# Low parts of the down weights by an adding DMA in a two-layer encoder on one core

## The chip, the core and the metric

The kernel runs on one core of a Trainium2 chip. The core has five engines that work side by side: TensorE (PE, matrix products), VectorE (DVE), ScalarE (ACT), GpSimd (POOL) and SyncE (SP), which here issues all DMAs; sixteen DMA engines move the bytes. The metric is device time in microseconds (us) of one execution; lower is better.

## The reference, cut to what matters

Two layers, each an FFN, a token-mixing sub-layer and a second FFN, on 256 tokens of width 1024, all in float32. The FFN:

```python
def swiglu(h, w_up, w_down):
    a, b = jnp.split(h @ w_up, 2, axis=-1)
    return (jax.nn.silu(a) * b) @ w_down          # w_up 1024 x 5632, w_down 2816 x 1024

for l in range(DEPTH):                            # DEPTH = 2
    h = rms_norm(x, ffn1_pre_g[l])
    x = x + 0.5 * rms_norm(swiglu(h, ffn1_w_up[l], ffn1_w_down[l]), ffn1_post_g[l])
    ...                                           # pooling, differential and memory attention, gates
    h = rms_norm(x, ffn2_pre_g[l])
    x = x + 0.5 * rms_norm(swiglu(h, ffn2_w_up[l], ffn2_w_down[l]), ffn2_post_g[l])
```

## The kernel before, in words

**Products in two parts.** PE multiplies in the type float32r, which keeps fewer bits of a number than float32. To lose little, every operand is split into a high part (the number rounded to float32r) and a low part (what the rounding left), and a product is the sum of high x high, high x low and low x high. So each weight has to become two tiles, `wh` and `wl`.

**Weights come in units.** All weights are packed on the host into 192 units of 128 x 2048 float32 (1 MB). `load_unit` (L99) issues a unit's DMA from SP into a tile `raw`, of which there are three buffers. `next_unit` (L103 and on) takes the oldest raw tile and makes the two parts, in two halves of 1024 columns each (four of 512 for the first five units of a stage): ACT writes the high part by a copy into float32r (L114), and DVE subtracts it from the raw weights to give the low part (L115). `wh` and `wl` have five buffers each. A raw buffer is free for the next load when both its readers are through; a weight buffer when PE has used the unit.

**The six stages.** FFN, mix, FFN for each layer. An FFN has 11 pairs of hidden columns (p = 0 to 10). For p from 2 on, the units of a pair's up weights come first (two units: `up2` at L241 for three of the stages; in the first stage `up`, L222), and then, for p = 2 to 9, the unit of the down weights of pair p - 2: `down(p - 2)`, whose products (L264, 24 of them in `rows_chunk`) are added up in four PSUM banks `acc`. So in the middle of a stage units come as up, up, down. The down units of the last three pairs come in the stage's `tail`, which ends in the norm and the residual.

**Beside the weights**, the hidden values go through ACT and DVE: `up2` copies a PSUM bank (L354), adds (L355), applies the gate function (L356), multiplies (L357) and splits the result into `hid` (L154, L155); the first stage does so by L330 and L331, PE transposes (L339), and L154, L155. In the first stage `ahead()` also prepares tables and the memory tokens (L410 to L513). POOL computes the power in the norms (L138).

**Order.** The program is written for a framework that sets semaphores by itself and plans the order of each engine's queue when the kernel is built; a few places are ordered by hand. Each engine works its queue in order: an instruction that waits holds up what stands behind it.

Of the kernel before, what the change touches and what calls it, by code (L numbers as in the profile page):

```python
# [9 lines left out]
F32 = mybir.dt.float32  # L10
F32R = mybir.dt.float32r
BF16 = mybir.dt.bfloat16
I32 = mybir.dt.int32
AF = mybir.ActivationFunctionType
ALU = mybir.AluOpType
# [30 lines left out]
def encoder_kernel(ctx, tc, x_d, xt_d, mem_d, memt_d, pos_d, w_d, gains_d, cols_d, lamv_d, poolw_d, cst_d, out_d):  # L46
    nc = tc.nc
# [15 lines left out]
    def acc_bank():  # L63
        return accp.tile([P, 512], F32, name="acc")
# [30 lines left out]
    def load_unit(parts=1):  # L95
        raw = rawp.tile([P, 2048], F32, name="raw")
        n = 2048 // parts
        for i in range(parts):
            nc.sync.dma_start(out=raw[:, i * n:(i + 1) * n], in_=w_d[nxt[0]][:, i * n:(i + 1) * n])  # L99
        nxt[0] += 1  # L100
        raws.append(raw)

    def next_unit():  # L103
        parts = 4 if fine[0] > 0 else 2
        fine[0] -= 1
        if not raws:
            load_unit()
        raw = raws.pop(0)
        h = wts.tile([P, 2048], F32R, name="wh")
        l = wts.tile([P, 2048], F32R, name="wl")  # L110
        n = 2048 // parts
        for s in range(parts):
            cs = slice(s * n, (s + 1) * n)
            high = nc.scalar.copy(out=h[:, cs], in_=raw[:, cs])  # L114
            low = nc.vector.tensor_tensor(out=l[:, cs], in0=raw[:, cs], in1=h.bitcast(F32)[:, cs], op=ALU.subtract)  # L115
            if nxt[1] < 2:
                first_low.append(low)
                first_high.append(high)
        nxt[1] += 1
        return h, l  # L120
# [133 lines left out]
    def rows_chunk(c, banks, todo, lhs_of, first, last):  # L254
        done = []
        for b in range(2):
            fs = slice(b * 512, (b + 1) * 512)
            for (w, kk) in todo:
                wh = w[0].rearrange("p (k m) -> p k m", k=2)
                wl = w[1].rearrange("p (k m) -> p k m", k=2)  # L260
                for k in range(2):
                    ah, al = lhs_of(c, kk, k)
                    for i, (a, ww) in enumerate(((ah, wh), (ah, wl), (al, wh))):
                        done.append(nc.tensor.matmul(  # L264
                            out=banks[b], lhsT=a, rhs=ww[:, k, fs],
                            start=(kk == first and k == 0 and i == 0),
                            stop=(kk == last and k == 1 and i == 2),
                        ))
        return done
# [14 lines left out]
    def ffn(i, xx, late, g_post, finish, ahead, raw_rstd=None):  # L284
# [9 lines left out]
            return hid[kk][0][:, c, k, :], hid[kk][1][:, c, k, :]  # L294

        def down(p):
            w = next_unit()
            if p == 0:
                for c in range(2):
                    acc[c] = [acc_bank(), acc_bank()]  # L300
            for c in range(2):
                rows_chunk(c, acc[c], [(w, p)], lhs_of, 0, NPR - 1)
# [42 lines left out]
        def up2(p, u):  # L345
            w = next_unit()
            banks = [ma_bank(), mb_bank()]
            for i in range(2):
                form_a2(banks[i], w, slice(i * P, (i + 1) * P), xx)
            flush()  # L350
            t = t2()
            for i in range(2):
                half = t[:, i * S:(i + 1) * S]
                nc.scalar.copy(out=half, in_=banks[i][:, S:2 * S])  # L354
                nc.vector.tensor_tensor(out=half, in0=banks[i][:, 0:S], in1=half, op=ALU.add)  # L355
            nc.scalar.activation(out=t[:, 0:S], in_=t[:, 0:S], func=AF.Silu)  # L356
            nc.vector.tensor_tensor(out=t[:, 0:S], in0=t[:, 0:S], in1=t[:, S:2 * S], op=ALU.mult)  # L357
            split(t[:, 0:S].rearrange("p (c t) -> p c t", c=2), hid[p][0][:, :, u, :], hid[p][1][:, :, u, :])

        ws = [(next_unit(), next_unit()) for _ in range(1 if raw_rstd else 2)]  # L360
        if raw_rstd:
            hs, ls = first_high, first_low
# [18 lines left out]
        for p in range(2, NPR):  # L381
            hid_pair(p)
            if raw_rstd:
                w2 = (next_unit(), next_unit())
                for c in range(2):
                    up(p, c, w2)
            else:
                for u in range(2):
                    up2(p, u)
            if p - 2 <= NPR - 4:  # L390
                down(p - 2)
            if p == 4:
                ahead()
# [529 lines left out]
```

## Time and profile before

| what | value |
|---|---|
| median of 3 runs | 1143.73 us (1143.53 to 1143.85) |
| the profiled execution | 1144.51 us, span in the trace 1142.5 us |
| granted TensorE clock, mean | 0.998 |
| PE busy | 1133.2 us, 99% of the span |
| DVE busy | 752.0 us, 66% |
| ACT busy | 626.8 us, 55% |
| POOL busy | 25.4 us, 2%, 37 instructions |
| DMA engines | 218.32 MB, mean 191 GB/s, busy 52.8% with the queue that SP feeds |

How to read it: the span is the time from the first to the last instruction in the trace; the execution's own time is about 2 us more. Busy time is what an engine spends in instructions, whether or not anyone waits for them. In the groups of the profile a row gives line, engine, operation, tiles and shapes, then the count, the busy time in us, the mean of one in ns, and the idle time of the engine just before them with what ended it. A "wait" names who waited for whom. DVE waits for the high part before 78 of its 444 subtractions, and SP's loads wait mostly for DVE, whose subtraction is the last reader of a raw buffer.

### The profile page before, as it was taken

The numbers are of one execution on the slowest core, as the hardware profiler recorded it, in microseconds if no ns is written. First come the engines' busy times: TensorE is split into PE (matmuls) and PEld (weight loads), VectorE is DVE, ScalarE is ACT, GpSimd is POOL, SyncE is SP. The second block draws the span as 40 slices with busy tenths as digits, with TensorE's granted clock in tenths as the row PEclk, the third lists the DMA queues.
The fourth block names the chain that finished last, engine by engine and source line by source line (L and its number), as shares of the span: only waits on it lengthen the run. The fifth ranks groups of instructions, "written<-read, shape, count | busy, mean of one in ns | idle before, by whom it ended". The sixth has DMA issues, their size and how long they took to land.

```text
span 1142.5 us, 14737 instructions
## 1 busy us (share of the span) xinstructions
PE 1133.2 (99%) x5679; PEld 947.5 (83%) x5679; DVE 752.0 (66%) x1164; ACT 626.8 (55%) x1121; POOL 25.4 (2%) x37
## 2 busy tenths in 40 slices
PE   8999999999999999999999999999999999999997
PEld 6888888887888888888888888888878888888886
DVE  6767456576768866566586756575677688666553
ACT  7666445545664555555565655555555646555551
POOL 0000000000000100000000000010000001000000
PEclk9999999999999999999999999999999999999999
DMA  8975553553454565555465655545545534655530
GB/s 314 341 245 223 192 188 139 211 189 120 170 205 161 212 249 195 196 184 185 148 234 208 221 188 186 185 163 202 183 147 188 199 149 171 253 184 184 185 111 37
DMA packets 35493, 218.32 MB, mean 191 GB/s; under 512 B 4192, under 2 KB 4448, under 8 KB 11232
## 3 DMA queue, kind: packets, MB, share of 16 engines
q1 hardware_dynamic: 35424, 217.40, 52.8%
q8 instruction: 44, 0.72, 0.2%
q14 instruction: 25, 0.20, 0.1%
HBM read 216.33 MB, written 1.05 MB: 190 GB/s over the span
## 4 chain that ended last, share of the span: by engine, by line
PE 98%; DVE 0%; DMA 0%; ACT 0%; issue 0%; SPq 0%; DVEq 0%; POOLq 0%; ACTq 0%
PE ma L222 37%; PE acc L264 25%; PE mb L241 13%; PE ma L241 13%; PE acc L222 2%; PE mb L222 2%; PE mb L197 1%; PE acc L617 1%; PE mb L339 1%; PE mb L495 1%; PE acc L634 1%; PE acc L675 1%; PE acc L660 1%; DMA raw<-in_w 0%; PE mb L748 0%; PE mb L560 0%
## 5 line engine op out<-in xcount | busy, mean ns | idle before, releaser
L115 DVE TENSOR_TENSOR wl<-raw,wh 128x1024 fp32r<-128x1024 f32 (+1 forms) x444 | 459.3, 1077 | 159.8 <-ACT wh L114 145.9
L114 ACT CAST wh<-raw 128x1024 fp32r<-128x1024 f32 (+1 forms) x444 | 391.5, 935 | 176.9 <-issue 102.0
L222 PE MATMUL ma<-wh,xhl 128*128 128x512 f32 x1184 | 379.6, 395 | 1.6 <-ACT wh L114 1.6
L222 PEld LDWEIGHTS ma<-wh,xhl 128*128 128x128 f32 x1184 | 221.9, 189 | 49.0 <-ACT wh L114 2.1
L222 PE MATMUL ma<-wl,xhl 128*128 128x512 f32 x592 | 233.1, 394 | 0.2 <-DVE wl L115 0.2
L264 PE MATMUL acc<-wh,hid 128*128 128x512 f32 x704 | 224.7, 391 | 0.0
L241 PE MATMUL ma<-xhl,wh 128*128 128x512 f32 x432 | 157.4, 398 | 0.0
L241 PE MATMUL mb<-xhl,wh 128*128 128x512 f32 x432 | 157.0, 397 | 0.0
L264 PEld LDWEIGHTS acc<-wh,hid 128*128 128x128 f32 x704 | 132.2, 188 | 26.2
L264 PE MATMUL acc<-wl,hid 128*128 128x512 f32 x352 | 137.1, 389 | 0.0
L222 PEld LDWEIGHTS ma<-wl,xhl 128*128 128x128 f32 x592 | 111.7, 189 | 23.8 <-issue 1.3
L241 PE MATMUL mb<-xhl,wl 128*128 128x256 f32 x432 | 112.5, 281 | 0.0
L241 PE MATMUL ma<-xhl,wl 128*128 128x256 f32 x432 | 112.4, 281 | 0.0
L241 PEld LDWEIGHTS ma<-xhl,wh 128*128 128x128 f32 x432 | 81.2, 188 | 15.8
L241 PEld LDWEIGHTS mb<-xhl,wh 128*128 128x128 f32 x432 | 81.5, 189 | 14.5
L355 DVE TENSOR_TENSOR s<-mb,s 128x256 f32<-128x256 f32 x54 | 22.9, 425 | 103.4 <-ACT s L354 103.4
L241 PEld LDWEIGHTS mb<-xhl,wl 128*128 128x128 f32 x432 | 81.6, 189 | 5.0
L241 PEld LDWEIGHTS ma<-xhl,wl 128*128 128x128 f32 x432 | 81.5, 189 | 4.6
L264 PEld LDWEIGHTS acc<-wl,hid 128*128 128x128 f32 x352 | 66.2, 188 | 13.7
L354 ACT COPY s<-mb 128x256 f32<-128x256 f32 x54 | 20.2, 373 | 58.4 <-PE mb L241 58.4
L356 ACT ACTIVATE s<-s 128x256 f32<-128x256 f32 x54 | 22.6, 418 | 50.9 <-DVE s L355 50.9
L138 POOL TENSOR_TENSOR sm<-sm,mhalf 128x1 f32<-128x1 f32 (+1 forms) x26 | 22.5, 865 | 1029.7 <-DVE sm L147 836.9
(162 smaller groups left out, 973.4 us busy)
## 6 DMA issues: line engine op xcount, KB each, us to landing
raw<-in_w SPq DMA_DIRECT2D x189, 1024.0 KB, 4.8
gain<-in_gains SPq DMA_DIRECT2D x17, 512.0 KB, 5.2
raw<-in_w SPq DMA_DIRECT2D x8, 256.0 KB, 5.5
hid<-in_memt SPq DMA_DIRECT2D x8, 256.0 KB, 5.7
hid<-in_xt SPq DMA_DIRECT2D x4, 256.0 KB, 5.3
raw<-in_w SPq DMA_DIRECT2D x2, 512.0 KB, 6.8
x<-in_x SPq DMA_DIRECT2D x4, 256.0 KB, 6.6
hid<-in_mem SPq DMA_DIRECT2D x4, 256.0 KB, 5.7
```

The source lines that it names most:

```text
L114: high = nc.scalar.copy(out=h[:, cs], in_=raw[:, cs])
L115: low = nc.vector.tensor_tensor(out=l[:, cs], in0=raw[:, cs], in1=h.bitcast(F32)[:, cs], op=ALU.subtract)
L138: nc.gpsimd.tensor_tensor(out=r, in0=v, in1=mhalf[:, :n], op=ALU.pow)
L197: tps.append(nc.tensor.transpose(out=ps[:, k * P:(k + 1) * P], in_=xn[:, i * P:(i + 1) * P], identity=ident))
L222: done.append(nc.tensor.matmul(out=out, lhsT=lhsT, rhs=rhs, start=(first and i == 0), stop=(last and i == n - 1)))
L241: nc.tensor.matmul(out=o, lhsT=ww[:, k, ms], rhs=rhs, start=(k == 0 and o is full), stop=(k == KT - 1 and o is full))
L264: done.append(nc.tensor.matmul(out=banks[b], lhsT=a, rhs=ww[:, k, fs], start=(kk == first and k == 0 and i == 0), stop=(kk == last and k = ...
L339: nc.tensor.transpose(out=tp[:, u * P:(u + 1) * P], in_=hn[:, u, :], identity=ident)
L354: nc.scalar.copy(out=half, in_=banks[i][:, S:2 * S])
L355: nc.vector.tensor_tensor(out=half, in0=banks[i][:, 0:S], in1=half, op=ALU.add)
L356: nc.scalar.activation(out=t[:, 0:S], in_=t[:, 0:S], func=AF.Silu)
L495: ins.append(nc.tensor.transpose(out=tp[:, i * P:(i + 1) * P], in_=a[:, hh, kt * P:(kt + 1) * P], identity=ident))
```

## The change

For the units that `down` fetches, 32 of the 192 (8 in each of the four FFN stages), the low part is made in another way. ACT writes the high part as before. Then ACT writes the negated high part into `wl` (a copy with scale -1), and POOL issues a DMA from `raw` to `wl`, SBUF to SBUF, that adds what it moves to what stands there. Each unit has two such halves of 128 x 1024 (512 KB). The down units of the tails, and all other units, keep the subtraction.

```diff
-    def next_unit():
+    def next_unit(added=False):
...
             high = nc.scalar.copy(out=h[:, cs], in_=raw[:, cs])
+            if added:
+                nc.scalar.activation(out=l[:, cs], in_=h.bitcast(F32)[:, cs], func=AF.Copy, scale=-1.0)
+                nc.gpsimd.dma_start(out=l[:, cs], in_=raw.bitcast(F32R)[:, cs], accum_op=ALU.add)
+                continue
             low = nc.vector.tensor_tensor(out=l[:, cs], in0=raw[:, cs], in1=h.bitcast(F32)[:, cs], op=ALU.subtract)
...
         def down(p):
-            w = next_unit()
+            w = next_unit(True)
```

## The prediction

> **What bounds the kernel now.** I read the page's busy times first, then its chain that ended last, then the longest pieces of that chain in order of time.
>
> ```profile
> span 1142.5 us, 14737 instructions
> PE 1133.2 (99%) x5679; PEld 947.5 (83%) x5679; DVE 752.0 (66%) x1164; ACT 626.8 (55%) x1121; POOL 25.4 (2%) x37
> PE 98%; DVE 0%; DMA 0%; ACT 0%; issue 0%; SPq 0%; DVEq 0%; POOLq 0%; ACTq 0%
> 0.00:7.40 7.40, 4.38 (x12) 1.52 (x12) 2.29 (x9) 4.00 (x8) 0.73 (x7) 1.00 0.65 197
> 1131.00:1142.50 11.50, 5.30 (x24) 4.05 (x22) 3.11 (x6) 1.38 (x4) 0.55 (x1) 0.92 0.24 91
> ```
>
> PE is idle for 1142.5 - 1133.2 = 9.3 us in all. The two windows (columns: length, then PE, PEld, DVE, ACT, POOL busy, clock, DMA share, GB/s) hold 3.0 us of it at the start and 6.2 us at the end, and neither stretch has a down unit that the change touches. Between them nearly nothing is left to win: a DVE that is 66% busy and behind no wait of PE can be relieved without shortening anything. So the question is only whether the longer way to a low part makes PE wait.
>
> **What the change takes away and adds.** `down` runs for p = 0 to 7 in each of four FFN stages: 32 units, two halves each, 64 halves. (The three down units of each tail call `next_unit()` without the flag.)
>
> ```profile
> L115 DVE TENSOR_TENSOR wl<-raw,wh 128x1024 fp32r<-128x1024 f32 x324 | 383.2, 1222 | 149.1 <-ACT wh L114 135.4 <-PE ma L222 8.9 <-issue 0.8
> L114 ACT CAST wh<-raw 128x1024 fp32r<-128x1024 f32 x324 | 325.2, 1052 | 171.3 <-issue 102.0 <-PE ma L222 45.6 <-PE acc L264 12.2
> q1 hardware_dynamic: 35424, 217.40, 52.8%
> raw<-in_w SPq DMA_DIRECT2D x189, 1024.0 KB, 4.8
> raw<-in_w SPq DMA_DIRECT2D x2, 512.0 KB, 6.8
> L138 POOL TENSOR_TENSOR sm<-sm,mhalf 128x1 f32<-128x1 f32 (+1 forms) x26 | 22.5, 865 | 1029.7 <-DVE sm L147 836.9 <-DVE sm L641 192.8
> L138 POOL TENSOR_TENSOR rmem<-sm,mhalf 128x1 f32<-128x1 f32 x2 | 1.1, 548 | 62.8 <-DVE sm L147 62.8
> ```
>
> DVE loses 64 x 1.22 = 78 us and ends near 674. ACT gains 64 sign flips; the nearest row is its cast of the same shape, 1.05 us, so 67 us, to 694. POOL gains 64 DMA issues. The DMA engines get 64 x 0.5 MB to write, and since an addition reads its target too, 1 MB to read for each half. None of these four sums is on PE's chain; what counts is the time from one unit's raw weights to its low part.
>
> Before, the second half of a unit is ready 3.44 us after its cast starts (below: 483.67 to 484.75 + 2.36). After, a unit takes four ACT passes of 1.05 us, 4.2 us, and then D: from the end of the last flip until the second addition has landed. No row shows D, so I bound it. The loads move 217.40 MB in 52.8% of 1142.5 us, so 1 MB (1.05 million bytes) costs all engines 2.9 us, and 4.8 - 2.9 = 1.9 us of a load is fixed. Lower end: an addition as cheap as a copy of half the bytes, 1.9 + 1.45, and 0.5 us of POOL time from its shortest row: D = 3.9 us. Upper end: the slowest landing of 512 KB in the page, 6.8 us, twice for the two reads, and the POOL row: D = 14.2 us. I take the bytes at face value: two reads of 512 KB go through the engines as 1 MB does, 4.8 us; POOL 0.9 us, its commonest row; and 0.8 us because the first half was issued only 2.1 us earlier and occupies the engines for 2.9. D = 6.5 us. This is nearest to the row of the 1 MB load, which runs 189 times, while the 6.8 row stands for two loads at the crowded start.
>
> A page weighs the same step: the Trainium skill, "Collectives: The Full Stack", section "The bandwidth ceiling: the fold count and why AG ≠ RS ≠ AR", says that the add in the DMA path costs no cycles of its own and that the second read halves the rate. By that rule D would stay at my 6.5 us; no run here shows it yet.
>
> **Where the unit stands in the steady stretch.** Units come as up, up, down; three raw buffers and five weight buffers. So a down unit always takes its raw buffer over from the down unit before it.
>
> ```profile
> 483.67 2.00 ACT L114 CAST wh<-raw 128x1024 fp32r<-128x1024 f32 x2
> 484.75 2.36 DVE L115 TENSOR_TENSOR wl<-raw,wh 128x1024 fp32r<-128x1024 f32 x2
> 487.14 0.33 SPq L99 DMA_DIRECT2D raw<-in_w  x1
> 500.38 2.00 ACT L114 CAST wh<-raw 128x1024 fp32r<-128x1024 f32 x2
> 489.00 5.45 PE acc L264 x24
> 505.72 5.45 PE acc L264 x24
> 480.00:520.00 40.00, 40.00 (x215) 34.35 (x214) 24.49 (x35) 21.17 (x35) 0.00 (x0) 1.00 0.52 186
> ```
>
> The cast at 483.67 starts when PE has left a unit and a weight buffer is free; its unit is used at 505.72 (the fifth unit on), and the second half's low part first by the fifth of its 24 matmuls, 4 x 5.45 / 24 = 0.9 us later. That is 23.0 us after the cast. The new way needs 4.2 + 6.5 = 10.7. Cover: 12.3 us, first test passed.
>
> Second test, the raw buffer. At 487.14 SP reloads it, right after the subtraction; the next cast from it is at 500.38, one period of 16.72 us after the last. After the change the round is 4.2 (ACT) + D + 4.8 (load) = 15.5 us at D = 6.5, inside 16.72; it breaks at D = 7.7. What is queued behind the new waits: on SP the load of the next unit, due a third of a period later at 487.14 + 5.6 = 492.7 and now held until 483.67 + 10.7 = 494.4, 1.7 us of the 500.38 - 487.14 - 4.8 = 8.4 that a load has to spare; on ACT the copies of PE's banks at L354, 2.1 us later, where a bank is written again only two units on, over 11 us; on POOL the norms' powers, not due before the tail. DMA share in this window is 0.52; two additions of 2.9 us per 16.72 add 0.35, to 0.87, still under 1.
>
> **Where it is tight: the first FFN stage**, where the buffers have just been filled.
>
> ```profile
> 34.54 0.33 SPq L99 DMA_DIRECT2D raw<-in_w  x1
> 33.14 2.01 ACT L114 CAST wh<-raw 128x1024 fp32r<-128x1024 f32 x2
> 36.81 0.33 SPq L99 DMA_DIRECT2D raw<-in_w  x1
> 42.91 5.47 PE acc L264 x24
> 59.74 5.47 PE acc L264 x24
> 34.00:40.00 6.00, 6.00 (x29) 4.95 (x28) 4.84 (x7) 4.11 (x7) 0.00 (x0) 1.00 0.96 373
> 90.97 0.47 ACT L330 ACTIVATE s<-ma,rst 128x256 f32<-128x256 f32 x1
> 91.48 0.48 DVE L331 SCALAR_TENSOR_TENSOR s<-ma,rst,s 128x256 f32<-128x256 f32 x1 [1.22 <-ACT s L330]
> 93.01 0.27 PE L339 MATMUL mb<-ident,s 128*128 128x128 f32 x1
> ```
>
> The first down unit is cast at 33.14, flipped by 37.3, and its second half is wanted at 42.91 + 0.9 = 43.8: D may be 6.5 at most, exactly what I estimate, while the engines are 0.96 busy with the load issued at 34.54. Sharing with that load costs up to half of one half's 2.9 us; I take 1.0 us of PE wait. The raw buffer, reloaded at 36.81 before, is now free at 44.8; the load lands at 49.6, the low part is there at 49.6 + 4.2 + 6.5 = 60.3, wanted at 59.74 + 1.0 + 0.9 = 61.6: passed by 1.3. From there the round of 15.5 against a period of 16.83 (59.74 - 42.91) gains 1.3 us each time. One more thin place: at 76 to 91 ACT works without a pause on the setup of tables and memory, and its L330 at 90.97 feeds, through DVE until 91.96, PE's transposes at 93.01: 1.05 us to spare against 2.1 us more ACT work, less what the earlier DVE subtractions free; I take 0.
>
> **Sum.** -0 (DVE off the path) + 1.0 (first down unit) + 0 (steady stretch, 30 units) = +1.0 us. The profiled execution took 1144.51 us, 2.0 over its span and 0.78 over the median of the three runs, 1143.73; I add to the median: 1144.7 us. About 0.2%, 2.3 us, is what a measurement of this kernel can tell from no change, so this is a forecast of no change.
>
> **Rivals.**
> Slow addition (the other side). If D is over 7.7, the raw round outgrows the period and the down units fall back by D - 7.7 a period. In the first stage there is no lead: at D = 10 it costs 3.5 + 7 x (10 - 7.8) = 18.9 us. In the other three the 23.0 us of cover hold 23.0 - 14.2 = 8.8 of the 7 x 2.3 = 16.1 us: 7.3 each, 22. Together +41, 1185 us. At D = 14.2: 7.7 + 44.8 in the first, 45.5 - 4.6 in the others, +175, 1319 us. It decides from D = 8, where the first stage costs about 3 us. For it: nothing in this profile shows an addition by DMA. Against: the engines have 0.48 of their time free in the steady window.
> Issue held up by DVE. POOL would write each transfer's orders only when DVE's running subtraction, 1.22 us, ends; two halves, 1.2 to 2.4 us, D = 7.7 to 8.9: 1.2 to 2.4 for the first unit and up to 7 x 1.1 behind it, +1 to +10, about 1150 us. The Trainium skill, "SBUF — State Buffer", section "SBUF: two separate sides", warns that a DMA issued from GpSimd waits while a two-port DVE operation holds the port they share. POOL here has 37 instructions, so the trace cannot say.
> Faster. The DVE wait behind ACT casts, or the thin place at 91, is relieved, and the queues fit together better. The price is bounded by PE's idle time outside start and end, 9.3 - 3.0 - 6.2 = 0.1 us, so 1143.6 us; below 1141.4 us it gets only if queues planned anew also shorten the start or the tail, and no row speaks for that.
>
> **How the numbers follow.** No change, D up to about 7.8: 0.54. Slow addition 0.33 (of it 0.14 beyond D = 10, which the range leaves out), issue held up 0.08, faster 0.05, mostly left out too. Half of the held-up case stays inside 0.2%, hence same 0.58, slower 0.37, faster 0.05. The range runs from 1142.5 (the median less somewhat more than the 0.78 us by which two executions differ here) to 1185 us, the slow addition at D = 10; the likeliest case's own range is 1142.5 to 1146.
>
> **What would show it.** Right: DVE near 674 us, ACT near 694, DMA queue of POOL with 64 transfers landing 5 to 7 us after issue; PE idle still about 10 us; in the list of waits PE's wait for low weights below 2 us, at the first down unit. Wrong: landings over 8 us, SP's reloads following the down units' additions by more than one period, and PE waits at L264 that recur every 17 us; or a longer wait of POOL's issues beside DVE work; or 24 matmuls of a down unit taking other than 5.45 us.

## The result, and the profile after

The changed kernel takes 1156.22 us (median of 4 runs, 1155.81 to 1156.71) against 1143.79 us for the kernel before, run beside it (1143.53 to 1144.93): a ratio of 1.0108, 95% interval 1.0093 to 1.0123. It is slower by 12.4 us. That lies in the range forecast, but the likeliest case, no change at 1144.7 us, did not happen. Of all runs behind this text one stands apart: one of the ten of only_first_held took 6493.76 us where the others took 1144.69 to 1145.12; it is left out of the ratios, and nothing on record explains it.

The page of the changed kernel, with the queue that POOL feeds, the new groups and the DMA issues (lines after the change stand 4 further down than before: L115 is now L119, L264 L268, L339 L343; L116 is the sign flip, L117 the adding DMA):

```profile
span 1154.9 us, 14883 instructions
PE 1137.9 (99%) x5679; PEld 948.3 (82%) x5679; DVE 679.7 (59%) x1100; ACT 681.9 (59%) x1185; POOL 81.1 (7%) x101
q0 software_dynamic: 9216, 33.56, 15.6%
L117 POOL DMA_DIRECT2D wl<-raw x64 | 55.6, 874 | 463.5 <-ACT s L358 297.3
wl<-raw POOLq DMA_DIRECT2D x64, 512.0 KB, 6.1
hid<-in_memt SPq DMA_DIRECT2D x8, 256.0 KB, 9.1
```

The edit itself does about what the prediction said: DVE 679.7 us (674 forecast), ACT 681.9 (694), 64 additions that land 6.1 us after issue (5 to 7). The memory tokens' loads (`hid<-in_memt`) take 9.1 us instead of 5.7. PE is idle for 1154.9 - 1137.9 = 17.0 us instead of 9.3, and 4.7 us of the growth is not idle at all: PE is *busy* that much longer with the same 5679 matmuls. The list of waits says where:

```profile
PE acc L268 <- DMA wl<-raw: 6.2, 2, 3.4
PE mb L343 <- DVE turns L446: 2.5, 1, 2.5
SPq L99 <- DMA wl<-raw: 336.6, 32, 15.6
```

PE issues its matmuls in the same order in all kernels here but for their line numbers, so the start of each can be set beside its partner in the kernel before. Where the delay grows (us, from these starts; "first unit" is the first down unit of the first FFN stage, before at 42.9; "setup" is the transposes at 93.0 and the 40 matmuls behind them):

| kernel | first unit | between | setup | all after it |
|---|---|---|---|---|
| changed kernel | +8.6 | 0.0 | +4.3 | +0.1 |
| late_stages | 0.0 | 0.0 | 0.0 | +0.1 |
| keep_first | 0.0 | 0.0 | +4.4 | +0.1 |
| only_first | +8.9 | 0.0 | 0.0 | 0.0 |
| only_first_held | +0.8 | 0.0 | 0.0 | 0.0 |
| all_held | +1.0 | 0.0 | +10.6 | +0.1 |
| all_held_skip | +1.0 | 0.0 | +7.5 | 0.0 |
| flip_then_dve | 0.0 | 0.0 | 0.0 | +0.1 |
| tokens_first | +1.0 | 0.0 | +0.8 | 0.0 |
| held_keep_two | +0.7 | 0.0 | 0.0 | 0.0 |
| copied | +2.3 | 0.0 | 0.0 | +0.1 |

(The profiled execution of the kernel before lost some 0.6 us in its first 30 us against most of the others; so the changed kernel's 8.6 + 4.3 + 0.1 stands beside a difference of 12.4 between the spans.) The whole loss lies at two places of the first FFN stage. Beside these two places the additions cost nothing.

**The first place.** In order of time, SP's issues, POOL's and PE's in the changed kernel (one view for each engine; columns: start, length, engine, line, operation, count, and the idle time before with what ended it):

```profile
33.97 0.33 SPq L99 DMA_DIRECT2D raw<-in_w  x1
34.34 0.42 SPq L414 DMA_DIRECT2D cst<-in_cst  x1
34.82 0.42 SPq L418 DMA_DIRECT2D pos_i<-in_pos  x1
35.28 0.67 SPq L87 DMA_DIRECT2D gain<-in_gains  x1
35.99 0.46 SPq L539 DMA_DIRECT2D pw<-in_poolw  x1
41.76 8.34 SPq L99 DMA_DIRECT2D raw<-in_w  x2
```

```profile
35.85 1.03 POOL L117 DMA_DIRECT2D wl<-raw  x1 [13.70 <-ACT wl L116]
38.71 0.88 POOL L117 DMA_DIRECT2D wl<-raw  x1 [1.83 <-ACT wl L116]
```

```profile
45.41 0.50 PE L268 MATMUL acc<-wl,hid 128*128 128x512 f32 x1 [2.81 <-DMA wl<-raw]
49.76 0.80 PE L268 MATMUL acc<-wl,hid 128*128 128x512 f32 x1 [3.40 <-DMA wl<-raw]
```

and SP's in the kernel before at the same time:

```profile
34.54 12.63 SPq L99 DMA_DIRECT2D raw<-in_w  x5
47.22 0.42 SPq L410 DMA_DIRECT2D cst<-in_cst  x1
```

SP's order is planned anew for the changed kernel. Where the next weight loads stood, at 36.81 and after, now stand four loads of the setup (cst, pos, a gain, pw; 304, 1, 512 and 128 KB); the next weight load comes behind them, at 41.76, since the plan now gives it the raw buffer of the unit after the first down unit, which DVE's subtraction leaves at 41.74. The four loads stand in the engines' queues when the addition is issued. The first addition's first row moves at 40.88, 4.0 us after POOL's issue ended (36.88), and in 3.3 of these 4.0 us the engines were carrying SP's transfers. The second shares with the weight load of 41.76 and is done at 49.41, 11.0 us after its flip.

**A pause costs more than its length.** Windows of the changed kernel, then of the kernel before (columns as in the prediction):

```profile
46.00:49.70 3.70, 0.37 (x2) 0.00 (x0) 0.00 (x0) 0.00 (x0) 0.00 (x0) 0.62 0.93 314
49.70:54.00 4.30, 4.24 (x11) 3.33 (x12) 0.00 (x0) 3.41 (x4) 0.17 (x1) 0.53 0.77 271
104.00:109.00 5.00, 5.00 (x17) 3.97 (x17) 1.52 (x6) 4.93 (x9) 0.00 (x0) 0.66 0.85 306
```

```profile
49.70:54.00 4.30, 4.30 (x22) 3.55 (x21) 2.36 (x2) 1.08 (x2) 0.00 (x0) 1.00 1.01 387
```

After the pause PE is busy all through 49.70 to 54.00, but at a granted clock of 0.53 it gets 11 matmuls done where 22 were done before. So the 6.2 us of waiting at the first unit become 8.6, and the 2.8 us at the transposes (L343: 2.5, and 0.3 more at its second pair) 4.3: these 3.9 us are most of the 4.7 by which PE is *busy* longer.

**The second place.** SP's issues in the changed kernel, then in the kernel before:

```profile
75.51 4.76 SPq L99 DMA_DIRECT2D raw<-in_w  x3
80.79 1.90 SPq L509 DMA_DIRECT2D hid<-in_mem  x4
82.74 9.27 SPq L517 DMA_DIRECT2D hid<-in_memt  x4
```

```profile
68.72 0.33 SPq L99 DMA_DIRECT2D raw<-in_w  x1
71.28 1.85 SPq L505 DMA_DIRECT2D hid<-in_mem  x4
73.18 7.47 SPq L513 DMA_DIRECT2D hid<-in_memt  x4
```

The memory tokens are loaded 9.5 us later (PE itself stands 8.1 us later there: the first loss, less what the kernel before had lost by itself), behind the same weight loads as before, which now bunch up. DVE's chain for the tables (to `turns`) and ACT's work on the tokens are planned one into the other, and the product that the transposes need stands behind both. Three of ACT's rows, then one of DVE's:

```profile
96.11 0.91 ACT L169 ACTIVATE xhl<-hid,colt 128x256 fp32r<-128x256 f32 x2 [2.35 <-DMA hid<-in_memt]
98.73 2.51 ACT L169 ACTIVATE xhl<-hid,colt 128x256 fp32r<-128x256 f32 x6 [1.71 <-DMA hid<-in_memt]
102.57 0.46 ACT L334 ACTIVATE s<-ma,rst 128x256 f32<-128x256 f32 x1
```

```profile
103.06 0.48 DVE L335 SCALAR_TENSOR_TENSOR s<-ma,rst,s 128x256 f32<-128x256 f32 x1
```

The transposes read the `s` of L335; the row of the wait names `turns` because that instruction of DVE ended last. L335 needs ACT's L334, and L334 stands in ACT's queue behind the work on the tokens, where ACT sits idle for their loads (5.7 us in all in this kernel, none in the kernel before). Why the tokens came late took the experiments.

### The profile page after: what moved, and what is told of

The parts are those of the page before. It is cut to its first block, busy times and chain, and to the rows that moved or that the text cites. A ratio compares the mean times of both kernels' runs of the same rounds, so it can differ in the third digit from the quotient of the medians.

```text
span 1154.9 us, 14883 instructions
## 1 busy us (share of the span) xinstructions
PE 1137.9 (99%) x5679; PEld 948.3 (82%) x5679; DVE 679.7 (59%) x1100; ACT 681.9 (59%) x1185; POOL 81.1 (7%) x101
## 3 DMA queue, kind: packets, MB, share of 16 engines
q0 software_dynamic: 9216, 33.56, 15.6%
HBM read 216.33 MB, written 1.05 MB: 188 GB/s over the span
## 4 chain that ended last, share of the span: by engine, by line
PE 92%; DMA 4%; ACT 1%; DVE 1%; issue 1%; POOL 0%; SPq 0%; DVEq 0%; POOLq 0%; ACTq 0%
PE ma L226 33%; PE acc L268 24%; PE mb L245 13%; PE ma L245 13%; PE mb L226 2%; PE acc L226 2%; DMA wl<-raw 2%; DMA hid<-in_memt 1%; DMA raw<-in_w 1%; PE mb L201 1%; PE acc L621 1%; ACT wh L114 1%; PE mb L499 1%; PE acc L638 1%; DMA hid<-in_xt 1%; PE mb L343 1%
## 5 line engine op out<-in xcount | busy, mean ns | idle before, releaser
L119 DVE TENSOR_TENSOR wl<-raw,wh 128x1024 fp32r<-128x1024 f32 (+1 forms) x380 | 383.9, 1051 | 151.4 <-ACT wh L114 139.6
L268 PE MATMUL acc<-wh,hid 128*128 128x512 f32 x704 | 227.3, 395 | 0.0
L268 PEld LDWEIGHTS acc<-wh,hid 128*128 128x128 f32 x704 | 133.9, 190 | 26.8
L268 PE MATMUL acc<-wl,hid 128*128 128x512 f32 x352 | 138.7, 394 | 6.2 <-DMA wl<-raw 6.2
L117 POOL DMA_DIRECT2D wl<-raw x64 | 55.6, 874 | 463.5 <-ACT s L358 297.3
L268 PEld LDWEIGHTS acc<-wl,hid 128*128 128x128 f32 x352 | 67.0, 190 | 20.8 <-DMA wl<-raw 7.0
L116 ACT ACTIVATE wl<-wh 128x1024 fp32r<-128x1024 f32 x64 | 67.3, 1059 | 0.0
```

What stands on the lines that cost most here:

```text
L116: nc.scalar.activation(out=l[:, cs], in_=h.bitcast(F32)[:, cs], func=AF.Copy, scale=-1.0)
L117: nc.gpsimd.dma_start(out=l[:, cs], in_=raw.bitcast(F32R)[:, cs], accum_op=ALU.add)
L268: done.append(nc.tensor.matmul(out=banks[b], lhsT=a, rhs=ww[:, k, fs], start=(kk == first and k == 0 and i == 0), stop=(kk == last and k = ...
```

## The experiments

All ratios are to the kernel before, run beside each. At the outset two theories stood against each other: the loss arises in the first stage alone, at its two places ("start"), or evenly over the 32 units, 0.39 us each ("spread").

**Three parts of the change alone.**

```diff
-            w = next_unit(True)
+            w = next_unit(raw_rstd is None)               # late_stages: stages 2 to 4
+            w = next_unit(raw_rstd is None or p > 0)      # keep_first: all but the first unit
+            w = next_unit(raw_rstd is not None and p == 0)  # only_first
```

> The adding DMA in the second to fourth FFN stage alone (24 units); the first stage keeps DVE's subtraction. Start theory (the whole 12.4 us arises in the first stage, in two waits, and the steady stretch hides everything): 1143.8 us, within 1 us of before, with no wait of PE for low weights at L268. Spread theory (each unit costs its share, 12.4 / 32 = 0.39 us, by a busier ACT and busier DMA engines): + 24 x 0.39 = 9.3, 1153 us.

> All down units but the very first one (p = 0 of the first stage) by the adding DMA. Start theory: the first wait and the slow matmuls behind it (8.3 us) are gone; the second one, in the setup of tables and memory (4.3 us), stays if it is of its own making: 1148 us; if it was an echo of the first, 1144. Spread theory: 31 / 32 of the loss stays, 1155.8 us.

> Only the very first down unit by the adding DMA, the other 31 by subtraction. Start theory: the first wait with its slow matmuls alone, + 8.3 us, 1152 us, and less or nothing at the setup. Spread theory: + 0.4 us, 1144.2.

Measured: late_stages 1144.33 us (1.0003, interval 0.9994 to 1.0013), keep_first 1149.16 (1.0047, 1.0032 to 1.0062), only_first 1152.92 (1.0077, 1.0062 to 1.0092). 24 of the 32 units cost nothing, and one unit alone costs 9 us: "spread" falls. The two losses are independent: each appears without the other.

**The first unit with the old order on SP.** The four setup loads are tied behind the load of unit 12, where they stood before.

```diff
+        held.append(nc.sync.dma_start(out=cst, in_=cst_d))     # and pos, the gain, pw
+            issue_after(held, mark[0])                         # mark: the load of unit 12
```

> As the one before, but four small loads of the setup (tables, positions, a gain, pool weights) are held back behind the load of the thirteenth weight unit, where they stood before the change. If the first addition was late because these loads, moved ahead, were queued in front of it (its first packet came 4.0 us after its issue had ended, elsewhere 0.6): PE's wait falls from over 6 to about 2 us and the time to 1146 to 1148 us. If the addition itself and the weight loads beside it are what is late: 1151 to 1153 us as without holding.

Measured 1144.87 us (1.0007, 0.9997 to 1.0016), below the 1146 to 1148 expected. PE's wait and the additions' median time from issue to landing, in only_first and then in only_first_held:

```profile
PE acc L268 <- DMA wl<-raw: 6.4, 2, 3.7
```

```profile
wl<-raw POOLq DMA_DIRECT2D x2, 512.0 KB, 10.2
```

```profile
PE acc L273 <- DMA wl<-raw: 0.5, 1, 0.5
```

```profile
wl<-raw POOLq DMA_DIRECT2D x2, 512.0 KB, 5.2
```

The same addition, issued at the same time, lands in 10.2 us behind the four setup loads and in 5.2 without them. The first loss is the queue's, shown by this one change.

**All units with that order, and one unit taken out.**

```diff
-            w = next_unit(True)                              # all_held: kept
+            w = next_unit(raw_rstd is None or p != 3)        # all_held_skip
```

> All 32 down units by adding DMA as in the changed kernel, but the four small setup loads (cst, pos, the third gain, pw) are held in SP's order behind the load of unit 12. Theory 'two collisions' (the 12.4 us are two separate losses, each an addition that has to wait in the queues behind other loads: 8.0 us at the first down unit because the setup loads were drawn ahead of it, 4.2 us before the transposes of the setup, where the memory tokens' loads and the fourth unit's additions share the engines): the first loss shrinks to about 1 us, as when only the first unit was added and these loads were held, the second stays: 1148 to 1149.5 us. Rival 'knock-on' (the second loss only follows from the first, which pushes everything behind it): both go, 1144 to 1145.5 us. Rival 'spread' (the time is lost in proportion to the number of additions): still over 1153 us.

> As the run with the four setup loads held, but the fourth down unit of the first stage (the one whose additions move at the same time as the memory tokens) keeps its DVE subtraction; 31 units are added. Theory 'two collisions': the second loss goes as well, 1144 to 1145.5 us. Rival 'ACT's load' (the setup before the transposes is late because ACT has 67 us more to do over the kernel, 4 units of it before this point, not because of transfers): three quarters of the second loss stay, 1147 to 1148.5 us.

Measured 1155.29 us (1.0093, 1.0078 to 1.0108) and 1153.51 (1.0076, 1.0060 to 1.0093). Both miss. The first loss went, as expected (PE's wait there 0.7 us); but the second did not stay at 4.3, it rose to 10.6, and in the second run to 7.5 although the unit that I blamed made no addition. That "spread" had said over 1153 is a coincidence of the sum: the table has all of it at the two places. So the fourth unit's additions are not the main cause. They may have a part in it: with them the last row of the tokens has moved at 95.60, without them at 91.05, and the loss is 3.1 us smaller. PE's waits of all_held and SP's issues there:

```profile
PE mb L348 <- DVE turns L451: 7.9, 1, 7.9
PE acc L273 <- DMA wl<-raw: 0.7, 1, 0.7
```

```profile
69.34 8.26 SPq L102 DMA_DIRECT2D raw<-in_w  x3
78.12 2.17 SPq L514 DMA_DIRECT2D hid<-in_mem  x4
```

SP issues a weight load at 69.34 and then stands until 76.79 at the next one (the row's 8.26 us take in both and a third), because an addition, the third down unit's, still reads that raw buffer. The token loads need no such buffer, but they stand behind it on SP: 78.12 where it was 71.28 before. In keep_first they were issued at 72.96, but directly behind two 1 MB loads.

**ACT's work without the DMA.** DVE adds the raw weights to what the flip wrote; no transfer is added.

```diff
-                nc.gpsimd.dma_start(out=l[:, cs], in_=raw.bitcast(F32R)[:, cs], accum_op=ALU.add)
+                nc.vector.tensor_tensor(out=l[:, cs], in0=raw[:, cs], in1=l.bitcast(F32)[:, cs], op=ALU.add)
```

> All 32 down units: ACT still writes the negated high part into the low part's buffer, but DVE adds the raw weights to it (in the place of its subtraction), with no DMA. ACT has the changed kernel's work, DVE the work of the kernel before, the queues are as before. Theory 'two collisions': no loss at either place beyond 0.5 us, 1143.8 to 1144.8 us. Rival 'ACT's load': the second loss (4 us) is there without any adding DMA, about 1148 us.

Measured 1144.18 us (1.0002, 0.9992 to 1.0011), with

```profile
PE 1132.6 (99%) x5679; PEld 946.0 (83%) x5679; DVE 750.2 (66%) x1164; ACT 684.2 (60%) x1185; POOL 25.7 (2%) x37
```

ACT does the changed kernel's 682 us and DVE nearly the old 752, and nothing is lost. The sign flips cost nothing here; the loss comes with the transfer and with the order that is planned for it.

**Putting the tokens ahead.** Two ways to undo the suspected order, both on top of all_held: the loads of units 16 and 17 behind the tokens, or the subtraction kept for the second and third down units, whose raw buffers those loads wait for.

```diff
+            if nxt[0] in (16, 17):                           # tokens_first
+                issue_after([ld], tokens[3])
...
-            w = next_unit(True)
+            w = next_unit(raw_rstd is None or p not in (1, 2))   # held_keep_two
```

> All 32 units by adding DMA, the four setup loads held behind the load of unit 12 as before, and now also the weight loads of units 16 and 17 held behind the last of the memory tokens' loads (SP: load of unit 15, lamv, 4 x mem, 4 x memt, then units 16 and 17). With the setup loads held, the wait before the setup's transposes was 8.4 us, and the token loads were issued 6.8 us later than in the kernel before (78.1 for 71.3), because SP stood 7.0 us at the load of unit 16, whose raw buffer an addition still read. Theory 'SP's order' (the second loss is this: SP issues in order, and the token loads stand behind a weight load that waits for an addition): the token loads go back to about 71 us and the loss shrinks to under 2 us (units 16 and 17 now come late, which may cost some of it): 1144 to 1147 us. Rival 'engines shared' (the second loss is additions and tokens sharing the 16 engines): it stays, over 1151 us.

> As the run with the setup loads held, but the second and third down units of the first stage (units 9 and 12, whose additions hold the raw buffers that the loads before the tokens take over) keep the DVE subtraction; 30 units are added. Theory 'SP's order': these raw buffers come free early again, the token loads are issued at 71 to 73 us, and the second loss is under 1.5 us: 1144 to 1146 us. Rival 'engines shared': the fourth unit's additions still meet the tokens, at least 4 us stay: over 1148 us.

Measured 1146.11 us (1.0017, 1.0007 to 1.0026) and 1145.80 (1.0015, 1.0005 to 1.0024). SP's issues of tokens_first and PE's waits at the second place, then those rows of held_keep_two:

```profile
68.94 0.33 SPq L102 DMA_DIRECT2D raw<-in_w  x1
71.44 2.04 SPq L516 DMA_DIRECT2D hid<-in_mem  x4
```

```profile
PE mb L350 <- DVE s L342: 1.0, 2, 0.6
```

```profile
71.45 1.94 SPq L514 DMA_DIRECT2D hid<-in_mem  x4
```

```profile
PE mb L348 <- DVE s L340: 0.4, 1, 0.4
```

With the tokens back at 71.4 the second loss falls from 10.6 to 0.8 and to 0.0 us, with all 32 additions in the first case and with the fourth unit's additions still there in both. "SP's order" holds, and "engines shared" falls as a cause by itself: in held_keep_two additions take 5.2 us of the engines' time between the tokens' first and last row, which ends at 86.32 instead of 81.97, and PE loses nothing, since the tokens come in time.

In the changed kernel's own order both meet. Against PE, SP issues the tokens only 1.4 us late (9.5 less 8.1). Their first row moves at 86.35, 5.6 us after the issue (in the kernel before at 72.78, 1.5 us after it), behind the three weight loads that SP issued from 75.51 on; and until their last row at 98.07 the additions (q0) share the engines with them, in the window 86.30:98.10:

```profile
q1 hardware_dynamic: 1182, 2.14, 56.3%
q0 software_dynamic: 287, 1.05, 44.5%
```

What each of the two makes of the 4.3 us no run separates.

With both orders put right, all 32 units by addition cost 2.1 us over the kernel before; no version here beats it. (held_keep_two has +0.7 in the table and +1.8 in its runs; in its profiled execution 1.3 us more than before lie behind the last matmul, and no run says why.)

**The limit of the steady stretch**, by doubling the addition in stages 2 to 4.

```diff
                 nc.gpsimd.dma_start(out=l[:, cs], in_=raw.bitcast(F32R)[:, cs], accum_op=ALU.add)
+                nc.gpsimd.dma_start(out=l[:, cs], in_=raw.bitcast(F32R)[:, cs], accum_op=ALU.add)
```

> FFN stages 2 to 4 only (24 units), and the adding DMA is issued twice for each half, so that the low part holds twice the raw weights less the high part. It doubles the suspected steady cost. In the run with one addition these stages lost nothing, at a DMA share of 0.82 in the second FFN stage's steady stretch. Theory 'engine share' (the stages have slack in D, and the bound is the 16 engines): two more occupations of 3.05 us in every 16.72 us make the share 0.82 + 0.37 = 1.19, so every unit takes about 3.1 us longer, 24 units 75 us: about 1220 us. Theory of the prediction's rotation of raw buffers: D = 6.5 + 2 x 3.05 = 12.6 us, 4.2 + 12.6 + 4.8 - 16.72 = 4.9 us per unit, 24 units 117 us: about 1260 us. Rival 'cover to spare': under 1150 us.

Measured 1244.26 us (1.0871, 1.0855 to 1.0888): 4.2 us for each of 24 units, between the two theories. The second FFN stage, in late_stages and then in twice_late, with two of the waits of its stretch from 405 to 590:

```profile
425.00:530.00 105.00, 105.00 (x554) 89.86 (x553) 51.84 (x77) 65.65 (x100) 10.46 (x12) 1.00 0.82 248
```

```profile
425.00:530.00 105.00, 91.55 (x446) 75.58 (x446) 39.04 (x59) 49.66 (x76) 16.31 (x19) 0.93 0.93 244
```

```profile
ACT wh L114 <- DMA raw<-in_w: 72.0, 23, 8.7
PE acc L269 <- DMA wl<-raw: 20.5, 10, 3.4
```

With one addition the engines are 0.82 busy and PE waits for nothing; with two they stay at 0.93, ACT waits for raw weights and PE for low parts. Part of the 4.2 us, over the 3.1 of the engines' share, is PE's clock, 0.93 in this window. How much, and how much is the raw buffers' round, these runs do not separate. From the packets, the last flip of a unit to its last row moved is about 19 us here, against 6.3 in late_stages: by the prediction's rule for the raw round it would have cost 21 x (19 - 7.7) = 237 us (7 rounds in each of 3 stages), with no cover left (23.0 - 4.2 - 19 is below 0). The rule overstates the price by more than twice.

**The price of the addition**, as a plain copy:

```diff
-                nc.gpsimd.dma_start(out=l[:, cs], in_=raw.bitcast(F32R)[:, cs], accum_op=ALU.add)
+                nc.gpsimd.dma_start(out=l[:, cs], in_=raw.bitcast(F32R)[:, cs])
```

> The changed kernel with a plain copying DMA in the place of the adding one (the low part is the raw weights, the high part is not subtracted; the sign flips stay). It prices the second read of the addition: if the addition's 3.05 us of engine occupation per half is twice a plain row because it reads the destination too, a copy's half takes 1.4 to 1.7 us (159 ns for a 4 KB row, 256 rows on 16 engines is 1.3 to 1.5 us per chunk of 128 x 2 rows), and the loss shrinks but does not go, since the same order on SP and the same issue remain: 1147 to 1152 us. If the cost is that of going through POOL's queue, with any operation, a half takes 3 us here too and the time is that of the changed kernel, 1155 to 1157 us.

Measured 1149.71 us (1.0050, 1.0035 to 1.0065):

```profile
q0 software_dynamic: 9216, 33.56, 8.1%
wl<-raw POOLq DMA_DIRECT2D x64, 512.0 KB, 3.1
```

```profile
PE acc L268 <- DMA wl<-raw: 1.8, 2, 1.2
```

The same rows take 8.1% of the engines' span as a copy and 15.6% as an addition: 0.081 x 1146.6 / 64 = 1.45 us a half, against 0.156 x 1154.9 / 64 = 2.8 (3.0, the median, from the first row of a half to the last). Landing takes 3.1 us instead of 6.1. (A half is 128 rows of 4 KB, 8192 rows in 64 halves, and not the 256 that the expectation counts: 8 rows of 159 ns on each engine are 1.3 us.) The first place still loses 2.3 us in the table, where the four setup loads are drawn ahead as in the changed kernel; the second loses nothing. This holds for the profiled execution, the fastest of the four, in which another 1.6 us lie behind the last matmul. Where the other three lose up to 3.4 us more, no trace tells.

## Why the prediction was right and wrong

The likeliest case failed at two of its terms, the first down unit and the setup. That the time still lies in the range is luck: the range reaches to 1185 us for slow additions, and slow additions are not what happened. Of the prediction's own signs, the landings of 5 to 7 us came; PE's wait for low weights was to stay below 2 us and was 6.2.

- **What bounds the kernel.** Right: DVE's 72 us less bought nothing, and in late_stages, with 24 of the 32 units changed, the ratio is 1.0003.
- **D.** Right: the prediction took 6.5 us; in the changed kernel's packets the median over 32 units is 6.3, 6.0 to 7.6 for most. The second read doubles the engines' time (2.8 us for 1.45), which agrees with what the Trainium skill, "Collectives: The Full Stack", section "The bandwidth ceiling: the fold count and why AG ≠ RS ≠ AR", says of a second read. The estimate of 2.9 stands. "Slow addition", at a chance of 0.33, fell.
- **Steady stretch, 0.** Right in its size: 0.0 in all columns after the setup, share 0.82 in the second stage (the estimate was 0.87). One step in it was wrong: "a down unit always takes its raw buffer over from the down unit before it" held in the kernel before only. The buffers go round anew in the plan of the changed kernel: in the first stage it is mostly the fourth load after a down unit's own, not the third, that takes its buffer. SP waits for an addition 32 times, up to 15.6 us, and in stages 2 to 4 PE notices none of it. The edge at D = 7.7 was not tried by itself: late_stages has one unit at 9.5 without any loss, which the prediction's own cover would also hold. Where D was far above it, in twice_late, the rule gave 237 us and 100 were lost.
- **Issue held up by DVE.** Fell: an issue takes 874 ns in the mean, the estimate's 0.9, with DVE at work beside it, and 28 of the 32 first halves move within 0.9 us of its end.
- **The first down unit, +1.0.** This is the first step that failed, by the factor 8.6. The step took the kernel before's queue on SP and let the addition share half with the load of 34.54. What the working lacked is that the order on SP is planned anew for the changed kernel: four setup loads were drawn ahead, cst by 12.9 us, and the addition began behind them. With the old order held the term measures +0.7 to +1.0. That this is what the working gave is two errors that cancel: the flips were not done by 37.3 but by 38.3 (38.4 in the changed kernel), since ACT's L158 and L334 were put between them, and D was 5.0 for 6.5 (only_first_held).
- **The setup, 0.** The second step that failed, by 4.3 us. It weighed ACT's additional work against 1.05 us to spare; flip_then_dve shows that this work costs nothing. It had the right chain, L330 and L331 before the transposes, but not the wait on it: ACT sat idle 5.7 us for the tokens. The step overlooked what stands *behind* a late weight load on SP: the token loads. The prediction asked what is queued behind a waiting load for the steady stretch alone (1.7 us on SP); asked for the first stage, the same question would have named them. In all_held the order on SP is shown to be the cause by the two runs that undo it; in the changed kernel the additions among the tokens' rows may have a share.
- **The clock.** No step had it: of 12.9 us in the table, 3.9 are not waiting but matmuls at about half the clock behind the two pauses.

## What to carry to other kernels

Here a slower way to make an operand was paid not where the operand is used most, but where buffers had just been filled, and through the queue. So list what stands behind each load whose buffer is now held longer, and what the planner will pull ahead of it. When a change loses time at a few places, tie the order of the old kernel back one load at a time; it tells the cost of the operation from the cost of the new plan. And price a PE pause above its length: here pauses of 2.5 us or more cost 1.2 to 2.4 us on top.

## What the runs showed of the hardware

- **In the changed kernel an addition issued on POOL began only when SP's earlier transfers were through, or nearly.** Of the 32 units' first halves in the changed kernel 28 had their first row moving within 0.9 us of the issue's end (second halves mostly wait for the first). Four came 1.5 to 4.4 us after it, and the engines carried SP's packets in nearly all of that time (3.29 of 4.00, 1.49 of 1.48, 4.10 of 4.36, 1.87 of 1.97 us). The Trainium skill, "DMA: Bandwidth & Descriptors", section "Queues, rings and completion order", says that an engine goes round between the queues with work, packet by packet; by that rule, with a row of the trace taken as a packet, the addition's rows would have moved between SP's from the start, and these four do not agree. The trace does not show what the engine counts as a packet, nor when the addition's orders stood in its queue, so this stays open.
- **The granted clock falls in a short pause.** After waits of 2.8 (changed kernel, setup), 6.2 (first unit, in two parts) and 8.3 us (all_held, setup) the matmuls behind lost 1.5, 2.4 and 2.3 us more, in the changed kernel at granted clocks of 0.66 and 0.53; after a wait of 0.7 us (all_held, first unit) the clock stayed at 1.0 and 0.3 us more were lost. The Trainium skill, "TensorE: Matmul & The Clock Gate", section "What's actually happening", has the clock at half after an idle window of about 3.4 us, until the array has been busy as long; the trace has half the clock from 46.91 to 53.74 and from 104.94 to 108.35, 6.8 and 3.4 us, which agrees. But 2.5 us without a matmul (101.23 to 103.69) was enough here, and there the clock fell only after PE had resumed.
- **The issue of an addition costs POOL 0.87 us, that of a copy of the same shape 0.54** (34.2 us in 64 issues of copied).
